# One early store of results split into four stores of 96, 14, 10 and 8 partitions

## The chip, the core and the metric

The kernel runs on one core of one Trainium2 chip. The metric is the device time of one execution in microseconds (us).

## The reference, cut to what matters

```python
x = np.random.randn(32, 512, 1024).astype(np.float32)   # 64 MiB
multiplier = 0.5

def reference(x, multiplier):
    return (np.sum(x, axis=-1) * multiplier).astype(np.float32)   # 32 x 512
```

Each row of 1024 numbers gives one number. Reading 67 MB is the work; the 64 KB of results are next to nothing.

## The kernel before

The 16384 rows are laid over 128 partitions, 128 rows each. Eight blocks of 16 rows per partition are loaded. The first 112 results of each partition form `out_rows`. The last block is loaded in shrinking pieces, so that little arithmetic is left once the last byte is in; its 16 results form `out_last`.

```python
    for b in range(n_blocks - 1):                   # 7 blocks, 8 MB each
        t = x_pool.tile([P, B, D], fp32, name="xb")
        loads.append(nc.sync.dma_start(out=t, in_=x_rows[:, c0 : c0 + B, :]))
        ...                                         # VectorE (and ScalarE) sum them into res
    pieces = [(0, 8), (8, 13), (13, 15)]            # the last block, in pieces
    ...
    for to, lo, hi in ((0, 0, cut), (at, cut, D)):  # its last row, in two parts
        loads.append(nc.sync.dma_start(out=end[:, to : to + hi - lo],
                                       in_=x_last[:, B - 1, lo:hi]))
    early = nc.sync.dma_start(out=out_rows, in_=res[:, 0:own])    # the early store, 56 KB
    ...                                             # sums of the last block
    first = dve_sum(end[:, 0:cut], end[:, at - 1 : at], 1.0)      # the last row, part one
    final = dve_sum(end[:, at - 2 :], res[:, rows - 1 : rows], mul)   # and the rest
    ...
    seen = nop_after(nc.sync, loads[-8:] + acts[-1:], [])
    store = nc.sync.dma_start(out=out_last, in_=res[:, own:])     # the last store, 8 KB
    ...
    nop_after(nc.sync, [early, final], [store])
```

Loads and stores all leave through SyncE's one DMA queue. The early store is issued when the results of the first seven blocks are there; by then the last loads have long been queued in front of it.

Of the kernel before, what the change touches and what calls it, by code (L numbers as in the profile page):

```python
# [1 line left out]

# [4 lines left out]


@with_exitstack
def kernel(  # L10
    ctx: ExitStack,
    tc: tile.TileContext,
    x: bass.AP,
    multiplier: float,
    out: bass.AP,
):











    nc = tc.nc
    P = nc.NUM_PARTITIONS
    fp32 = mybir.dt.float32  # L30
    ADD = mybir.AluOpType.add

    x_flat = x.flatten_outer_dims()
    N, D = x_flat.shape
    rows = N // P
    out_flat = out.rearrange("b s -> (b s)")
    mul = float(multiplier)

    B = 16
    n_blocks = rows // B  # L40
    assert N == P * rows and rows == n_blocks * B
    own = rows - B
    x_rows = x_flat[0 : P * own, :].rearrange("(p c) d -> p c d", p=P)
    x_last = x_flat[P * own : N, :].rearrange("(p c) d -> p c d", p=P)
    out_rows = out_flat[0 : P * own].rearrange("(p c) -> p c", p=P)
    out_last = out_flat[P * own : N].rearrange("(p c) -> p c", p=P)

    x_pool = ctx.enter_context(tc.tile_pool(name="x", bufs=3))
    res_pool = ctx.enter_context(tc.tile_pool(name="res", bufs=1))
    sums = res_pool.tile([P, rows], fp32, name="sums")  # L50
    res = res_pool.tile([P, rows], fp32, name="res")
    cut = 576
    at = 608
    end = res_pool.tile([P, at + D - cut], fp32, name="end")
    nc.vector.memset(end[:, at - 2 : at], 0.0)  # L55

    SYNC = mybir.DependencyInfo(mybir.DependencyClass.Sync, mybir.DependencyReason.DATA)
    ORDER = mybir.DependencyInfo(
        mybir.DependencyClass.NoSync, mybir.DependencyReason.SCHED_ONLY
    )  # L60

    def nop_after(engine, waits_for, follows):
        i = engine.nop()  # L63
        for w in waits_for:
            tc.add_manual_dep(i.ins, w.ins.name, SYNC, reason="end seen here")
        for f in follows:
            tc.add_manual_dep(i.ins, f.ins.name, ORDER, reason="in this order")
        return i

    loads = []  # L70
    acts = []

    def act_row(t, r, col):
        acts.append(nc.scalar.activation(  # L74
            out=t[:, r, :],
            in_=t[:, r, :],
            func=mybir.ActivationFunctionType.Copy,
            scale=mul,
            accum_out=res[:, col : col + 1],
        ))  # L80

    def dve_sum(row, dst, scale):
        mid = row.shape[-1] // 2
        return nc.vector.tensor_tensor_reduce(  # L84
            out=row[:, 0:mid],
            in0=row[:, 0:mid],
            in1=row[:, mid:],
            scale=scale,
            scalar=0.0,
            op0=ADD,  # L90
            op1=ADD,
            accum_out=dst,
        )

    for b in range(n_blocks - 1):
        c0 = b * B
        t = x_pool.tile([P, B, D], fp32, name="xb")
        loads.append(nc.sync.dma_start(out=t, in_=x_rows[:, c0 : c0 + B, :]))  # L98
        h = B if b < n_blocks - 2 else B // 2
        nc.vector.reduce_sum(  # L100
            out=sums[:, c0 : c0 + h], in_=t[:, 0:h, :], axis=mybir.AxisListType.X
        )
        nc.vector.tensor_single_scalar(  # L103
            out=res[:, c0 : c0 + h],
            in_=sums[:, c0 : c0 + h],
            scalar=mul,
            op=mybir.AluOpType.mult,
        )
        for r in range(h, B):
            act_row(t, r, c0 + r)  # L110

    c0 = (n_blocks - 1) * B
    t = x_pool.tile([P, B, D], fp32, name="xb")
    pieces = [(0, 8), (8, 13), (13, 15)]
    for lo, hi in pieces:
        loads.append(
            nc.sync.dma_start(  # L117
                out=t[:, lo:hi, :], in_=x_last[:, lo:hi, :]
            )
        )  # L120
    for to, lo, hi in ((0, 0, cut), (at, cut, D)):
        loads.append(
            nc.sync.dma_start(
                out=end[:, to : to + hi - lo], in_=x_last[:, B - 1, lo:hi]
            )
        )
    early = nc.sync.dma_start(out=out_rows, in_=res[:, 0:own])
    on_act = {4, 5, 6, 7, 11, 12, 14}
    for r in range(B - 1):
        if r in on_act:  # L130
            act_row(t, r, c0 + r)
        else:
            dve_sum(t[:, r, :], res[:, c0 + r : c0 + r + 1], mul)
    first = dve_sum(end[:, 0:cut], end[:, at - 1 : at], 1.0)
    part_seen = nop_after(nc.vector, [first], [])
    final = dve_sum(end[:, at - 2 :], res[:, rows - 1 : rows], mul)

    tc.add_manual_dep(final.ins, part_seen.ins.name, ORDER, reason="in this order")
    tc.declare_no_dep(final.ins, first.ins.name, reason="waited for by the nop in front")




    seen = nop_after(nc.sync, loads[-8:] + acts[-1:], [])
    store = nc.sync.dma_start(out=out_last, in_=res[:, own:])
    tc.add_manual_dep(store.ins, seen.ins.name, ORDER, reason="in this order")
    for a in acts[-len(on_act) :]:
        tc.declare_no_dep(store.ins, a.ins.name, reason="waited for by the nop in front")
    nop_after(nc.sync, [early, final], [store])

    def start_loads_at_entry(nc_):



        entry, *rest = nc_.main_func.blocks
        is_sp = lambda i: i.engine == mybir.EngineType.SP
        is_load = lambda i: type(i).__name__ == "InstDMACopy"
        for block in rest:
            body = list(block.instructions)
            own = [i for i in body if is_sp(i)]  # L160
            if not any(is_load(i) for i in own):
                continue
            lead = []
            for i in own:
                if not is_load(i) or i.sync_info.on_wait:
                    break
                lead.append(i)
            names = {i.name for i in lead}
            block.instructions = [i for i in body if i.name not in names]
            head = list(entry.instructions)  # L170
            at = next(
                k for k, i in enumerate(head) if is_sp(i) and type(i).__name__ == "InstDrain"
            )
            entry.instructions = head[:at] + lead + head[at:]
            return

    nc.at_finalize(start_loads_at_entry)


# [1 line left out]
_INS = ['x', 'multiplier']  # L181
_OUTS = [((32, 512), 'float32')]

_NUMBERS = {'multiplier': 0.5}


# [26 lines left out]
```

## Time and profile before

| What | Before |
|---|---|
| Time, median of 3 runs | 162.17 us (162.13 to 162.17) |
| Span in the profile | 160.2 us |
| DMA engines' busy share of the span | 97.6% |
| Last load piece landed | 157.52 us |
| Early store issued, landed | 147.74, 157.73 us |
| Last store issued, landed | 158.04, 159.47 us |

How to read it: the span is what the profile covers; the measured time is some 2 us longer. "Landed" is the moment when the last DMA engine has counted up the completion semaphore (a semaphore is a counter that an engine can wait for; a count on it is called an increment here). The lines themselves stand in the prediction.

### The profile page before, as it was taken

The page shows a single profiled execution, that of the slowest core. Times are in us where ns is not written, and L with a number is a line of the kernel's source. Part 1 is how long each engine was busy: PE and PEld are TensorE (multiplying, and loading weights), DVE is VectorE, ACT ScalarE, POOL GpSimd, SP SyncE. Part 2 cuts the span into 40 slices and gives each one's busy share as a digit, 9 for nine tenths or more (in the row PEclk, how much of TensorE's full clock was granted, in tenths as well). Part 3 has the DMA queues.
Part 4 walks back from the last instruction along what each step waited for, and adds up shares of the span by engine and source line. Part 5 has one row for each costly group of instructions (what it writes and reads, how often), then busy time and mean ns, then how long its engine had stood idle before and what let it go on. Part 6 is the DMA issues. An engine that isn't in the chain of part 4 may idle for free.

```text
span 160.2 us, 139 instructions
## 1 busy us (share of the span) xinstructions
DVE 119.3 (74%) x35; ACT 17.3 (11%) x31; POOL 0.2 (0%) x4
## 2 busy tenths in 40 slices
DVE  0000059997799968999599995999959999597443
ACT  0000000000000000000000000000000000599952
POOL 0000000000000000000000000000000000000000
DMA  7996996996996996997998979969969969999992
GB/s 262 524 524 262 524 524 262 524 524 262 524 524 262 524 491 295 524 458 327 524 409 376 524 344 442 524 262 524 524 262 524 524 262 524 393 393 425 409 410 81
DMA packets 2016, 67.18 MB, mean 419 GB/s; under 512 B 480, under 2 KB 608, under 8 KB 736
## 3 DMA queue, kind: packets, MB, share of 16 engines
q1 hardware_dynamic: 2016, 67.18, 97.6%
HBM read 67.11 MB, written 0.07 MB: 419 GB/s over the span
## 4 chain that ended last, share of the span: by engine, by line
DMA 75%; DVE 22%; SPq 1%; issue 0%; DVEq 0%
DMA xb<-in_x_dram 51%; DMA end<-in_x_dram 24%; DVE sums L100 22%; SPq L117 1%; DVE end L84 1%; SPq L98 0%; DVE res L103 0%; DVEq L63 0%; DVEq L208 0%
## 5 line engine op out<-in xcount | busy, mean ns | idle before, releaser
L100 DVE TENSOR_REDUCE sums<-xb 128x16 f32<-128x16384 f32 (+1 forms) x7 | 112.0, 16001 | 31.5 <-DMA xb<-in_x_dram 31.5
L74 ACT ACT_TABLE_LOAD x1 | 1.3, 1283 | 138.0 <-DMA xb<-in_x_dram 138.0
L74 ACT ACTIVATE xb<-xb 128x1024 f32<-128x1024 f32 x15 | 15.7, 1044 | 2.1 <-DMA xb<-in_x_dram 2.1
L84 DVE CUSTOM_DVE_ANT_0 xb<-xb 128x512 f32<-128x512 f32 x8 | 5.1, 688 | 5.0 <-DMA xb<-in_x_dram 5.0
L74 ACT ACTIVATION_READ_ACCUMULATOR xb<-xb 128x1 f32 x15 | 2.8, 186 | 0.0
L55 DVE MEMSET end<- 128x2 f32 x1 | 0.1, 60 | 1.8 <-PEq L194 1.8
L103 DVE TENSOR_SCALAR res<-sums 128x16 f32<-128x16 f32 (+1 forms) x7 | 1.2, 174 | 0.2
L84 DVE CUSTOM_DVE_ANT_0 end<-end 128x288 f32<-128x288 f32 (+1 forms) x2 | 0.9, 426 | 0.2
L84 DVE DVE_READ_ACCUMULATOR2_ANT res<- 128x1 f32 x9 | 0.7, 82 | 0.0
L194 POOL MEMSET const-bfloat16-1.0<- 128x1 bf16 x1 | 0.1, 102 | 0.0
L194 POOL MEMSET const-uint8-127<- 128x1 uint8 x1 | 0.1, 101 | 0.0
L194 POOL MEMSET const-float32-0.0<- 128x1 f32 x1 | 0.1, 99 | 0.2 <-issue 0.2
L194 POOL MEMSET const-float32-1.0<- 128x1 f32 x1 | 0.1, 98 | 0.0
L84 DVE DVE_READ_ACCUMULATOR2_ANT end<- 128x1 f32 x1 | 0.1, 82 | 0.0
## 6 DMA issues: line engine op xcount, KB each, us to landing
xb<-in_x_dram SPq DMA_DIRECT2D x1, 4096.0 KB, 31.1
xb<-in_x_dram SPq DMA_DIRECT2D x1, 2560.0 KB, 36.8
xb<-in_x_dram SPq DMA_DIRECT2D x1, 1024.0 KB, 38.9
end<-in_x_dram SPq DMA_DIRECT2D x1, 288.0 KB, 39.1
end<-in_x_dram SPq DMA_DIRECT2D x1, 224.0 KB, 39.1
xb<-in_x_dram SPq DMA_DIRECT2D x7, 40.8
out_dram<-res SPq DMA_DIRECT2D x1, 56.0 KB, 10.0
out_dram<-res SPq DMA_DIRECT2D x1, 8.0 KB, 1.4
```

Source lines behind the costliest of these rows:

```text
L55: nc.vector.memset(end[:, at - 2 : at], 0.0)
L74: acts.append(nc.scalar.activation(out=t[:, r, :], in_=t[:, r, :], func=mybir.ActivationFunctionType.Copy, scale=mul, accum_out=res[:, col ...
L84: return nc.vector.tensor_tensor_reduce(out=row[:, 0:mid], in0=row[:, 0:mid], in1=row[:, mid:], scale=scale, scalar=0.0, op0=ADD, op1=ADD, ...
L100: nc.vector.reduce_sum(out=sums[:, c0 : c0 + h], in_=t[:, 0:h, :], axis=mybir.AxisListType.X)
L103: nc.vector.tensor_single_scalar(out=res[:, c0 : c0 + h], in_=sums[:, c0 : c0 + h], scalar=mul, op=mybir.AluOpType.mult,)
L117: nc.sync.dma_start(out=t[:, lo:hi, :], in_=x_last[:, lo:hi, :])
L194: nc = _bacc.Bacc("TRN2", target_bir_lowering=False, num_devices=1)
```

## The change

The intent: a store of 128 partitions runs on all 16 DMA engines, 8 rows on each. Stores of 96, 14, 10 and 8 partitions run on 16, 14, 10 and 8 engines. By the rule that the prediction quotes, small engine counts fall on the low-numbered engines (the traces name no engine numbers), so engines 0 to 7 should get 9 rows, 8 and 9 should get 8, 10 to 13 should get 7, and 14 and 15 only 6.

```diff
-    early = nc.sync.dma_start(out=out_rows, in_=res[:, 0:own])
+    early = []
+    p0 = 0
+    for n in (96, 14, 10, 8):
+        early.append(
+            nc.sync.dma_start(out=out_rows[p0 : p0 + n], in_=res[p0 : p0 + n, 0:own])
+        )
+        p0 += n
...
-    nop_after(nc.sync, [early, final], [store])
+    nop_after(nc.sync, early + [final], [store])
```

## The prediction

> **What bounds the kernel now.** I read the page's busy shares and slices first, then the chain that ended last, then the DMA issues with the SyncE waits, and last the windows over the final microseconds, because the change touches only stores. The page of the kernel before says what fills the span (the digits are busy tenths in 40 slices):
>
> ```profile
> span 160.2 us, 139 instructions
> DVE 119.3 (74%) x35; ACT 17.3 (11%) x31; POOL 0.2 (0%) x4
> DMA  7996996996996996997998979969969969999992
> DMA packets 2016, 67.18 MB, mean 419 GB/s; under 512 B 480, under 2 KB 608, under 8 KB 736
> q1 hardware_dynamic: 2016, 67.18, 97.6%
> ```
>
> The 16 DMA engines are busy for 97.6% of their time, moving 67 MB of input. No compute engine comes near. Only the last slice is thin: there the load stream is over and a short tail runs. The tail stands in the chain of waits in order of time (start, length, what):
>
> ```profile
> 117.89 39.08 DMA end<-in_x_dram
> 156.97 0.02 issue
> 156.99 0.48 DVE end L84 x2
> 157.47 0.03 issue
> 157.50 0.02 DVEq L63
> 157.52 0.09 issue
> 157.61 0.39 DVE end L84
> 158.00 0.01 DVEq L208
> ```
>
> The last load pieces land at 156.97 (the first part of the last row) and 157.52 (the second part, in the trace's landing records). Two short vector sums follow and the last result is written at 158.01. So the end is: load stream, two sums, one store of 8 KB, closing barrier. The early store, which the change splits, is not a link in it. Where it does stand is in the DMA issues (KB, microseconds from issue to landing) and in the waits of SyncE's queue:
>
> ```profile
> end<-in_x_dram SPq DMA_DIRECT2D x1, 224.0 KB, 39.1
> out_dram<-res SPq DMA_DIRECT2D x1, 56.0 KB, 10.0
> out_dram<-res SPq DMA_DIRECT2D x1, 8.0 KB, 1.4
> SPq L63 <- DMA end<-in_x_dram: 9.4, 1, 9.4
> SPq L208 <- DMA out_dram<-res: 1.0, 1, 1.0
> ```
>
> The timeline has the early store issued at 147.74, taking 0.35 us on SyncE, and the last one at 158.04. So the early one lands at 147.74 + 10.0 = 157.74, the last one at 158.04 + 1.4 = 159.47. SyncE waits 9.4 us for the end loads between the two, and after the last issue it waits 1.0 us on the last store alone. The windows show what the DMA engines do then (us, busy DVE, ACT, POOL, clock, DMA share, GB/s):
>
> ```profile
> 149.50:156.97 7.47, 3.30 (x12) 5.41 (x11) 0.00 (x0) 1.00 0.95 392
> 156.97:158.04 1.07, 0.87 (x4) 0.42 (x2) 0.00 (x0) 1.00 0.11 29
> 158.04:160.20 2.16, 0.00 (x0) 0.00 (x0) 0.00 (x0) 1.00 0.04 4
> ```
>
> From 156.97 on the DMA share is 0.11 and then 0.04: the engines are nearly idle where the early store's data moves.
>
> **What the Trainium skill says.** First, "DMA: Bandwidth & Descriptors", section "Why a DMA increments its semaphore by 16 and not by 1": a DMA from SyncE uses the largest k up to 16 that divides the slowest dimension, on the lowest-numbered k engines, and the sequencer writes the missing 16 - k increments itself. That gives 16, 14, 10 and 8 engines for this change, as intended. The trace before has 16 increments for every 128-partition DMA; it names no engine numbers and has no smaller k, so no run here shows that part yet. Second, the same page, "Queues, rings and completion order": on each engine one issuer's descriptors are consumed in ring order. The trace agrees: 56 KB issued at 147.74 landed only at 157.74, just behind the last load piece at 157.52, and its first 448-byte packet starts at 156.75. Third, "Perfetto Trace Analysis", section "DMA Instruction — HWDGE (DVE, Sync)": the profiled window of a DMA instruction holds descriptor generation and the sequencer's own increments, not the data. The trace agrees: 0.35 us of instruction against 10.0 us to landing. Fourth, the DMA page's "Specifications" asks for at least 512 B per transfer for line rate; the rows here are 448 B before and after, so the change doesn't touch that.
>
> **The change part by part.** The build order shows one difference: one store of 128x112 becomes four, of 96, 14, 10 and 8 rows; vector and scalar queues are unchanged.
>
> Removed and added on SyncE: three more DMA instructions. SyncE's issues back to back take 0.33 to 0.48 us each (timeline: 1.35 us for three, 0.92 for two), with 0.05 between them. Four take 4 x 0.48 + 3 x 0.05 = 2.1 us at most, so SyncE is done by 149.8 instead of 148.1. The second to fourth also wait for a semaphore that a load used before, by the build order; those loads landed at 137.9, 137.9 and 147.62, all before 147.74. Then SyncE would wait for the end loads anyway, until 157.52. Slack 7.7 us: cost on the path 0.
>
> On the DMA engines: with k as above, engines 0 to 7 write 6 + 1 + 1 + 1 = 9 rows, engines 8 and 9 write 8, engines 10 to 13 write 7, engines 14 and 15 write 6 (72 + 16 + 28 + 12 = 128). Before, each wrote 8. In the packet records 448-byte packets of one engine start 21 ns apart and a semaphore packet takes another 6 or so. Busiest engine: 9 x 21 + 4 x 6 = 213 ns against 8 x 21 + 6 = 174, so +0.04 us. Lightest: 6 x 21 + 6 = 132, so -0.04. The slowest engine ends its early data at 157.27 before; it will end between 157.23 and 157.31. The next packet in the records, the first of the last store, starts at 158.88. So the engines stand idle for 1.6 us in between, and 0.04 either way vanishes there.
>
> The landing: four stores by 157.7 to 157.8 instead of one by 157.74. Nobody waits for that until SyncE has issued the last store at 158.38.
>
> The waits at the end: in front of the last store the build lists the same semaphores as before; these waits ended at 157.73, and the store waited for the vector result until 158.01. Behind it, SyncE must see three more stores. Its semaphore instructions follow each other every 0.06 us (157.57, 157.64, 157.70), so 3 x 0.06 = 0.2 us more, from 158.43 to 158.7, inside the 1.0 us that it waits for the last store till 159.47. The closing barrier (159.48 to 160.22) is as before. Cost 0.
>
> Sum: 0 removed from the path, 0 added. 162.17 + 0.0 gives about 162.2; I put the centre at 162.2.
>
> **The rivals.** (a) The intended gain: if the engines that finish loading last were numbers 14 and 15, and the end hung on the early store, giving these two rows less would bring it forward. For: the engines do end unevenly (the semaphore packets of the last load spread from 156.74 to 157.05). Against: the chain passes through the vector sums, not the store, and the gain is bounded by 2 x 21 = 42 ns. Time 162.13, no more than the spread of the runs.
>
> (b) The stores disturb the loads. In the packet records, packets of 20,480 B normally take 761 ns, but 20 of those that start between 149 and 151 us take together 1.43 us longer: 1.43 / 16 = 0.09 us per engine. That begins 1.4 us after the early store is issued. If each issue does this, four cost up to 0.36 instead of 0.09 us: +0.27, so 162.45. Against: the five issues between 116.5 and 118.8 are followed by only 0.46 us in excess, 0.03 per engine, so the coincidence may be chance. I give it one in six.
>
> (c) A new wait takes the place of the old: the last store held until all four early ones have landed, or the three added waits checked only after the last landing. The first would cost nothing while they land by 157.8 (the store goes at 158.04); the second 0.2 us: 162.35. The build order speaks against both.
>
> (d) Small k makes a store slow, since each engine's increment must follow its own write to memory: before, the landing came some 0.46 us after an engine's semaphore packet. Four such in a row, not overlapped, would be 1.8 us: early data would be complete at 157.27 + 1.8 = 159.1, still before 159.47 where the last store lands, unless that store's increments queue behind them, for some 0.3 us more. Against: consecutive load pieces, with semaphore packets between them, run on with no gap.
>
> **Range and chances.** The core case (no change, about three in four) gives the spread of the runs, 162.13 to 162.17, widened to about 0.15 either side since a rebuilt program can settle a little differently (the profiled run was 162.0). Rivals (b), (c) and (d) stretch the upper end by 0.2 to 0.3; (a) the lower by 0.04. So 161.9 to 162.5. Two per cent is 3.2 us, more than ten times the largest rival, and no part of the tail that the change touches has that much: the whole from the last load to the end is 160.22 - 157.52 = 2.7 us. Faster 0.004, slower 0.011, same 0.985.
>
> **What would show it right or wrong.** Right: four early issues between 147.7 and 149.9; the last row's sums still start within 0.1 us of 156.99 and 157.61; the last store still goes about 0.43 us after the second sum's start and lands 1.4 us later; four early landings before 158; more small packets by 3 sets of semaphores (14 + 10 + 8 = 32, so 2048 packets). For (a): the end loads or the last store earlier. For (b): the end loads land 0.1 us or more later, with long packets after 148. For (c): the last issue waits for the stores, or more than 0.05 us between its landing and the closing barrier. For (d): early landings after 158.5. The prediction is wrong if the time leaves 161.9 to 162.5, most likely through a slower load stream, the only thing here that is long enough.

## The result, and the profile after

The changed kernel took 162.19 us (median of 4 runs, 162.03 to 162.38), the kernel before 162.15 us beside it (4 runs, 162.07 to 162.17). The ratio is 1.0004, with a 95% interval of 0.9987 to 1.0021: the same. Ratios are the mean time of one kernel's runs over that of the other's of the same rounds, so they are not quite the ratio of the medians quoted.

The page after, in the lines that answer to those of before:

```profile
span 160.2 us, 143 instructions
...
DMA  7996996996996996997989979979969969999992
...
DMA packets 2048, 67.18 MB, mean 419 GB/s; under 512 B 512, under 2 KB 640, under 8 KB 768
...
q1 hardware_dynamic: 2048, 67.18, 97.4%
```

The span and the 67.18 MB have not moved. There are 2048 packets instead of 2016: the 32 new ones are the completion increments of the three smaller stores (14 + 10 + 8), packets of 4 bytes. The chain that ended last, in order of time (start, length, what):

```profile
118.34 39.24 DMA end<-in_x_dram
157.58 0.06 issue
157.63 0.39 DVE end L84
158.03 0.01 DVEq L214
```

It ends as before in a load, the second vector sum and the last store. It names the second part of the last row (landed at 157.58) where the chain of before named the first part (156.97) and went through both sums; the two routes end within 0.1 us of each other in both profiles, so that is no new bound. SyncE's issues in the timeline (start, length to the end of the last of the group), and its waits (us, times, longest):

```profile
147.78 1.53 SPq L131 DMA_DIRECT2D out_dram<-res  x4
158.06 0.36 SPq L151 DMA_DIRECT2D out_dram<-res  x1
```

```profile
SPq L63 <- DMA out_dram<-res: 8.2, 1, 8.2
...
SPq L214 <- DMA out_dram<-res: 0.9, 1, 0.9
```

Four issues take 1.53 us. The wait of 8.2 us needs care: it says that SyncE waited for a store, where the profile of before said 9.4 us for the end loads. The instruction's record holds two semaphores. One counts the last load piece. The other counted an earlier load and is now shared with the third early store, which is where the name comes from. The wait ended at 157.60, just behind the load's landing at 157.58, while that store landed only at 158.08. It is still the wait for the load. The 0.9 us behind the last store is that store's own landing, as before. Last, the DMA issues (KB, us to landing):

```profile
out_dram<-res SPq DMA_DIRECT2D x1, 42.0 KB, 10.0
out_dram<-res SPq DMA_DIRECT2D x1, 6.1 KB
out_dram<-res SPq DMA_DIRECT2D x1, 4.4 KB
out_dram<-res SPq DMA_DIRECT2D x1, 3.5 KB
out_dram<-res SPq DMA_DIRECT2D x1, 8.0 KB, 1.4
```

The page gives no landing for a store on fewer than 16 engines. The trace's semaphore records do: the three have 14, 10 and 8 increments by DMA engines and one more update, at 148.78, 149.16 and 149.49, just behind the end of each issue and long before the data moves, so by the sequencer. That agrees with the rule for the number of engines that the prediction quotes. The four landings are at 157.76, 157.87, 158.08 and 158.28. In a second profile of the same kernel they are at 157.69, 157.82, 157.90 and 158.07. All are well before 159.49, where the last store lands.

### The profile page after: what moved, and what is told of

It is laid out like the page before. It is cut to its first block, busy times and chain, and to the rows that moved or that the text cites. A ratio compares the mean times of both kernels' runs of the same rounds, so it can differ in the third digit from the quotient of the medians.

```text
span 160.2 us, 143 instructions
## 1 busy us (share of the span) xinstructions
DVE 119.3 (74%) x35; ACT 17.3 (11%) x31; POOL 0.2 (0%) x4
## 2 busy tenths in 40 slices
DMA packets 2048, 67.18 MB, mean 419 GB/s; under 512 B 512, under 2 KB 640, under 8 KB 768
## 3 DMA queue, kind: packets, MB, share of 16 engines
q1 hardware_dynamic: 2048, 67.18, 97.4%
## 4 chain that ended last, share of the span: by engine, by line
DMA 75%; DVE 22%; SPq 1%; issue 0%; DVEq 0%
DMA xb<-in_x_dram 51%; DMA end<-in_x_dram 24%; DVE sums L100 22%; SPq L117 1%; SPq L123 0%; SPq L98 0%; DVE end L84 0%; DVE res L103 0%; DVEq L214 0%
```

## The experiments

The theory (A) is the prediction's: the early store's data moves in an idle stretch between the end of the loads and the last store, and nothing waits for it there. Its rivals are that issuing stores disturbs the loads (B), and that completion of several small stores in a row is slow enough to matter. Eleven runs were made, three of them repeats of a kernel. The first four shared 9 runs of the kernel before (median 162.05), the second four 9 others (162.03), the last three 7 (162.00).

### The changed kernel again

No edit.

> The changed kernel once more, for a tighter interval. Theory A (nothing waits for the early stores, the engines stand idle for 1.6 us behind them): ratio to before between 0.999 and 1.001, about 162.15 us. Theory B (issuing four stores beside the loads delays the load stream by up to 0.27 us): ratio 1.001 to 1.002, about 162.4 us, and long 20,480-byte packets between 148 and 151 us in the profile. The two spreads are compared as well: single runs of the changed kernel went from 162.03 to 162.38.

Measured: 162.01 us (5 runs, 161.90 to 162.16), ratio 0.9998 (0.9984 to 1.0012). The wider spread of the first four runs did not return, and 20,480-byte packets that start between 148 and 151 us were 0.04 us too long in total. Theory B with four issues costing 0.27 us (ratio 1.0017) lies outside this interval.

### Without the early store

```diff
-    early = nc.sync.dma_start(out=out_rows, in_=res[:, 0:own])
...
-    nop_after(nc.sync, [early, final], [store])
+    nop_after(nc.sync, [final], [store])
```

> The early store is left out, so 112 of the 128 columns of results are never written and the output is wrong on purpose. This is the most that any change of the early store could gain. Theory A: 162.1 us, ratio 0.999 to 1.001, with the end loads landing at 157.0 and 157.5 as before. If the store's issue or its 8 rows per engine cost something on the path (theory B for one issue: 0.09 us; the rows: 8 x 21 ns = 0.17 us), the time falls by 0.1 to 0.26 us, ratio 0.9984 to 0.9994.

Measured: 161.97 us (5 runs), ratio 0.9998 (0.9986 to 1.0011). Its output is wrong, which doesn't matter for the time. The chain of this kernel (start, length, what):

```profile
156.91 0.03 issue
156.93 0.48 DVE end L84 x2
...
157.55 0.40 DVE end L84
157.95 0.01 DVEq L207
```

Taking the store away altogether gains nothing that the clock shows, so no way of splitting it could gain more than the interval leaves open, 0.14% or 0.2 us. This is the ceiling that settles the question of the change. The interval does not exclude all of the 0.1 to 0.26 us that the store might have cost by the expectation. The traces resolve a little more than the clock. From the landing of the last block's first piece to that of the last load piece it takes:

| Early store | us, each profile |
|---|---|
| none | 9.86, 9.86 |
| one of 128 partitions (before) | 9.90, 9.91 |
| 96, 14, 10 and 8 (the change) | 9.92, 9.91 |
| four of 32 | 9.96 |
| 127 and 1 | 9.86 |
| 122 and 6 | 9.85 |
| one of 128, on ScalarE's queue | 9.98 |

So a store that is spread over many engines behind the loads seems to cost the loads some 0.04 to 0.1 us, whether split or not, which is at most 0.06% of the time. The two stores that are nearly all on one or two engines, in runs further down, show no such cost. With one or two profiles for each row this is an indication, not more.

### Four equal stores

```diff
-    for n in (96, 14, 10, 8):
+    for n in (32, 32, 32, 32):
```

> Four early stores of 32 partitions each, so all on 16 engines, 2 rows per engine and store: the number of stores of the changed kernel with the balance of the kernel before. In the changed kernel the four landed at 157.76, 157.87, 158.08 and 158.28. If the number of completion increments on one engine sets that (about 0.1 to 0.2 us each), the last of these four lands at 158.2 to 158.4 here as well. If the smaller number of engines per store sets it, the last lands by 157.9. The time is 162.2 us under both, as nothing waits for them until 158.5.

Measured: 162.10 us (4 runs), ratio 1.0001 (0.9987 to 1.0014). The landings: 157.83, 158.00, 158.18 and 158.39, so 0.17, 0.18 and 0.21 us apart, and the last inside the range expected for the first reading. In the changed kernel they were 0.11, 0.20 and 0.20 apart, and 0.13, 0.08 and 0.17 in its second profile. The data is not what takes the time: the last 448-byte packet of this kernel starts at 157.45. So the number of stores, each with a completion increment of its own on an engine, sets the late landings; the smaller engine counts don't.

### All rows on one engine, behind the loads

```diff
-    for n in (96, 14, 10, 8):
+    for n in (127, 1):
```

> Two early stores of 127 and 1 partitions. 127 has no divisor from 2 to 16, so by the rule of the Trainium skill all 127 rows run on one engine. Theory A with its sizes: 127 rows x 21 ns = 2.7 us on an engine that ends its loads at about 156.6 to 156.9, so its rows end at about 159.3 to 159.6, past 158.88 where the last store's packets start; that engine's part of the last store then lands at about 159.8 to 160.1 instead of 159.47, and the time is 162.5 to 162.9 us. If the early store never matters to the end, 162.2 us. If small writes are slower when one engine has them all, or the queue of that engine fills and blocks the issuing queue, more: over 163.5 us.

Measured: 163.47 us (4 runs, 163.34 to 163.71), ratio 1.0089 (1.0075 to 1.0103). The early store can matter, then. Lines of the timeline, of the waits and of the DMA issues of this kernel:

```profile
147.82 9.60 SPq L131 DMA_DIRECT2D out_dram<-res  x2
```

```profile
SPq L63 <- DMA out_dram<-res: 2.5, 1, 2.5
```

```profile
out_dram<-res SPq DMA_DIRECT2D x1, 8.0 KB, 3.0
```

Behind the last store SyncE now waits 2.5 us for the early stores, and the last store takes 3.0 us to land instead of 1.4, since one engine has to finish its early rows first: 15 of its 16 increments land by 159.51, the last at 161.14. The second issue is blocked for 9.2 us (the sequencer's record: from 148.18 to 157.42); it comes free just before SyncE needs it. The size was expected too small, in three terms. The busy engine's first row starts at 157.12, not at 156.6 to 156.9, for it was one of the last two to end their loads. Its 128 rows take 3.0 us, where 2.7 were expected for 127: the first 60 start 21 ns apart, the others 26 on average. And its increments land one after the other at 160.77, 160.96 and 161.14, so the last comes 0.92 us behind the last data packet (160.22), where the kernel before needs 0.4.

### All rows on two engines

```diff
-    for n in (96, 14, 10, 8):
+    for n in (122, 6):
```

> Two early stores of 122 and 6 partitions: by the rule, 61 rows on each of two engines, then one row on each of six. Theory A with the sizes of the run with 127 rows on one engine (21 ns a row at first): 62 rows end about 1.3 us after that engine's loads, at 158.2 to 158.4, before the last store's packets at 158.9. So the slack still covers it: 162.05 us, ratio 0.999 to 1.0015, while the early landings move out to 158.9 to 159.2. If imbalance costs in proportion, half of the 1.4 us that one engine cost: 162.7 us, ratio 1.004.

Measured: 161.96 us (4 runs), ratio 0.9993 (0.9979 to 1.0006). Two lines of SyncE's waits:

```profile
SPq L63 <- DMA end<-in_x_dram: 3.7, 1, 3.7
...
SPq L63 <- DMA out_dram<-res: 0.7, 1, 0.7
```

The last early row starts at 158.27 and the early stores land at 158.87 and 159.05, over a microsecond later than in the kernel before, and SyncE does wait 0.7 us for them. The last store still lands at 159.46, and the time is unchanged. This brackets the slack: with 61 or 62 rows on an engine it is not used up, with 128 it is. The change moves one row, from 8 to 9, on the engines that get more.

### The same single store on ScalarE's queue

```diff
-    early = nc.sync.dma_start(out=out_rows, in_=res[:, 0:own])
+    early = nc.scalar.dma_start(out=out_rows, in_=res[:, 0:own])
```

> The single store of the kernel before, issued on the scalar engine's DMA queue instead of the one that has the loads in front of it. Theory A says that the store is free because its ring puts it behind the loads, into idle time. On its own queue it should be served between load packets and land before 151 us instead of 157.7; the 8 rows (8 x 21 = 0.17 us per engine) then stand ahead of the end of the loads: the end loads land 0.15 to 0.2 us later, 162.2 us, ratio 1.0005 to 1.002. If small stores are hidden wherever they go: ratio 1.000. If they disturb the loads beyond their own time: over 1.003.

Measured: 162.16 us (5 runs, 162.09 to 162.20), ratio 1.0004 (0.9992 to 1.0017). Of the DMA issues and the chain:

```profile
out_dram<-res ACTq DMA_DIRECT2D x1, 56.0 KB, 7.9
```

```profile
157.77 0.39 DVE end L84
158.16 0.01 DVEq L208
```

The store landed at 155.74, before the loads ended, but not before 151 as expected: its first packet starts at 151.39, 3.6 us behind the issue. Why so late was not examined. The loads of this profile end 0.12 us later than without a store (9.98 against 9.86 in the table), somewhat under the 0.15 to 0.2 expected. The time's interval covers both that and no loss, so by the clock alone this run decides nothing.

### 127 rows on ScalarE's queue

```diff
-    for n in (96, 14, 10, 8):
+    for n, q in ((127, nc.scalar), (1, nc.sync)):
...
-            nc.sync.dma_start(out=out_rows[p0 : p0 + n], in_=res[p0 : p0 + n, 0:own])
+            q.dma_start(out=out_rows[p0 : p0 + n], in_=res[p0 : p0 + n, 0:own])
```

> 127 rows in one store on the scalar engine's queue (so all on one engine, and not behind the loads), the last row on the old queue. If one engine serves the store's rows between its load packets with no limit, 127 x 21 to 26 ns = 2.7 to 3.3 us come ahead of the loads of one engine, the end loads land 2.7 to 3.3 us later and the time is 164.8 to 165.4 us. If it takes turns, a few small packets for each load packet of 0.76 us, only part goes ahead and the rest follows the loads: 162.3 to 164 us. If the place in the queue doesn't matter, the same 163.5 us as with 127 rows behind the loads.

Measured: 163.23 us (4 runs), ratio 1.0071 (1.0056 to 1.0086): the second reading. By the clock alone it can hardly be told from the 163.47 us of 127 rows behind the loads, for the intervals of the two ratios overlap; the packet records decide. They show the turns: while the engine has load packets, the store's rows start 0.327 us apart between packets of 8,192 B, each followed by a row 0.306 us after its own start, and 0.11 and 0.09 us apart between the smaller ones. So one row of 448 B goes for one load packet. Only some 30 of the 127 rows had gone by 157.56, when the rows begin to follow each other at 21 ns, and the last load piece landed at 157.89 instead of 157.52.

### The change's split where the engines are the bound

```diff
-    for to, lo, hi in ((0, 0, cut), (at, cut, D)):
-        loads.append(
-            nc.sync.dma_start(
-                out=end[:, to : to + hi - lo], in_=x_last[:, B - 1, lo:hi]
-            )
-        )
+    for to, lo, hi in ((0, 0, cut), (at, cut, D)):
+        p0 = 0
+        for n in (96, 14, 10, 8) if to == 0 else (P,):
+            loads.append(
+                nc.sync.dma_start(
+                    out=end[p0 : p0 + n, to : to + hi - lo],
+                    in_=x_last[p0 : p0 + n, B - 1, lo:hi],
+                )
+            )
+            p0 += n
```

> The change's split (96, 14, 10, 8) applied to the first part of the last row's load, where the DMA engines are the bound, with the early store whole as before. In one profile of the changed kernel the two engines that finished loading last had the row pattern of numbers 14 and 15. If these are always last, 2 rows less (2 x 93 ns) let the end loads land up to 0.1 us earlier: ratio 0.999. The three further completion increments, about 0.2 us each on the engines that carry all four, delay the landing of that part by 0.2 to 0.6 us, and the first of the two end sums waits for it: 162.2 to 162.6 us, ratio 1.001 to 1.003. I expect the second to win.

Measured: 163.02 us (5 runs, 162.81 to 163.36), ratio 1.0061 (1.0048 to 1.0073), so worse than expected. Its chain:

```profile
157.88 0.03 issue
157.90 0.05 DVEq L84
157.95 0.08 issue
158.04 0.48 DVE end L84 x2
```

The first sum of the last row starts at 158.04 instead of 156.99. The last of the four loads landed at 157.88 instead of 156.97, and VectorE's further semaphore instructions take the rest. Not all of this delay arises in the split load: the piece in front of it (rows 13 and 14 of the block) had already landed at 156.64 instead of 156.22. The packets are longer as well: those of 2,304 B took 116 ns on average instead of 94, those of 1,792 B behind them 113 instead of 74.

As a check of where the longer packets come from, the same with four equal parts:

```diff
-        for n in (96, 14, 10, 8) if to == 0 else (P,):
+        for n in (32, 32, 32, 32) if to == 0 else (P,):
```

> Like the run that split the first end load into 96, 14, 10 and 8 partitions and took 163.0 us, but with four loads of 32, so all on 16 engines with 2 rows each. There the 2,304-byte packets took 116 ns on average instead of 94 and the 1,792-byte packets behind them 113 instead of 74. If the smaller number of engines (another assignment of partitions to engines) lengthens the packets, they take 94 and 74 here and the time is 162.3 to 162.6, only the increments and the vector engine's three further waits being left. If four loads in a row cost that in any form, 162.9 to 163.1 as there.

Measured: 162.83 us (4 runs, 162.67 to 163.21), ratio 1.0051 (1.0026 to 1.0076). The packets took 130 and 103 ns, and the piece in front landed at 156.57, so it is not the smaller engine counts alone that lengthen the packets: four loads of parts of the partitions do it with 16 engines too. What in them does stays open. The time lies just under the 162.9 to 163.1 us expected for that case. No kernel tried beats the kernel before by the clock.

### Second profiles with and without the early store

No edit in the first; the second is the kernel without the early store again.

> The kernel before, a second profile. In its first profile 20 packets of 20,480 B between 149 and 151 us took 1.43 us longer together; with four stores one profile had 2.2 us of that and two had under 0.1. If the burst belongs to the store, it is here again with 1 to 2 us; if it comes and goes by itself, it may be absent, and the time is 162.0 to 162.2 in either case.

> Without the early store (output wrong on purpose), a second profile. The first had no long packets between 148 and 151 us. If the burst needs a store, none here either; if it comes and goes by itself, one may appear. One time of 161.9 to 162.2 us.

Measured: 161.98 and 162.08 us, one run each. The kernel before has the burst of long packets again, 2.7 us in total between 148 and 151 us where 1 to 2 were expected, and the kernel without the store has none again. The four-store changed kernel had under 0.1 us in both of its profiles, and the four equal stores 2.2 us. So the burst wants a store, but not every store brings it, and more issues don't bring more of it; of the two runs with a split load, which have a single early store of 128 partitions, the one with 96, 14, 10 and 8 had 2.4 us and the one with four equal loads 0.2. What makes it is open. It costs little: the load stream from the table is as long with it (9.90, 9.91) as in the changed kernel without it (9.92, 9.91). On which engines it falls was not looked into.

## Why the prediction was right, point by point

The time of 162.19 us lies on the predicted 162.2, and most steps held. That the two agree to 0.01 us is chance: the four runs went from 162.03 to 162.38, and the next five had a median of 162.01, still inside the range of 161.9 to 162.5.

**The bound and the path.** The early store is in no link of the chain in either profile, and the run without it shows nothing to gain. The last row's sums started at 157.02 and 157.63, within the 0.1 us that was allowed.

**SyncE's issues.** At most 2.1 us, done by 149.8, were predicted; they took 1.53 us, done by 149.32 (0.36, 0.46, 0.29 and 0.29 us), with 8 us of slack. One reading was wrong without effect: the semaphore of the second store had last counted a load that landed at 118.6, not 137.9.

**Rows per engine and idle time behind them.** The last increment packet of the early data starts at 157.21 after and at 157.27 before; 157.23 to 157.31 was predicted, so it is early by 0.02 us. The next packets start at 158.92. Nothing of it reaches the end. The two runs with very uneven stores put the limit of this idle time between 62 and 128 rows on one engine.

**The landings: this step failed.** The prediction's "four stores by 157.7 to 157.8" and "four early landings before 158" were wrong: the last was at 158.28 in the first profile and 158.07 in the second. It had counted one further increment as a packet of 6 ns. As landings, the increments of one engine follow each other some 0.1 to 0.2 us apart, as the four equal stores confirm. That they come one after the other is what rival (d) supposed, but with 0.46 us each, so that its sign, landings after 158.5, did not appear. Whether the wait for an engine's own write spaces them, as (d) has it, no run here shows. As nothing waits for these landings before the last store's own, the error cost nothing.

**The waits.** In front of the last store they ended at 157.79, before the vector result at 158.04. Behind it the added ones ended at 158.63, before 159.49. Both were as worked out, and rival (c) is out.

**The rivals.** (a), the intended gain: in the changed kernel's first profile the two engines that ended their loads last do show the packet pattern of engines with only six early rows, which numbers 14 and 15 have by the rule. In the second profile the last engine shows it too, and the last but one has another pattern. So the change does relieve late engines at times, and their store rows still gate nothing. (The spread of the ends of the loads in the kernel before was read as 156.74 to 157.05; its last load packets start at 157.03 and their semaphore packets at 157.10.) (b): more long packets with more issues did not appear.

## What to carry to other kernels

Before balancing a transfer over the DMA engines, ask what waits for its end: here a store queued behind the last loads lands in time that the final arithmetic and the last store leave idle. The quickest test is to leave the transfer out (wrong output and all), which shows the ceiling of any rearrangement; loading one engine until it shows then gives the slack. Splitting a transfer was not free where something does wait for it: the split end load cost 0.5 to 0.6%.

## What the Trainium skill lacked or had wrong

- "DMA: Bandwidth & Descriptors", section "Why a DMA increments its semaphore by 16 and not by 1": the rule for the number of engines agrees (14, 10, 8, 2 and 1 increments by engines for stores of 14, 10, 8, 122 and 127 partitions). It gives no rate for increments that follow each other; the runs show small stores behind each other landing 0.08 to 0.21 us apart while their rows start 21 ns apart.
- The same page, section "Queues, rings and completion order": it calls a turn between queue rows a whole packet of typically some 9 to 17 descriptors. With 448-byte rows beside loads the runs show one row per turn: row starts 0.327 us apart, of which the load packet takes 0.306, from its start to the next row's.
- "Perfetto Trace Analysis", section "DMA Instruction — HWDGE (DVE, Sync)": it has a wait for a lock inside the profiled window and a descriptor buffer that can fill, but no word on how long an issue can be held. The one-row store behind 127 rows on one engine spent 9.2 us in its issue and the six-row store behind 122 rows on two engines 5.6 us, against 0.3 to 0.5 us for the stores of the changed kernel. What exactly held them no run shows.
